# Two plain feed-forward tiles ahead of the Strassen products, sums of token blocks moved behind them

## The chip, the cores and the metric

The kernel runs on one core of a Trainium2 chip. The metric is the device time of one execution in microseconds (us); the median of three runs before the change is 2620.79 us (2618.11 to 2621.23).

## The reference

Two trunk layers of a diffusion backbone, for 128 context tokens and 512 latent tokens (640 columns in all), with a model width of 1024. Each layer is

```
x += 1/2 * gate1 * SwiGLU_1(mod(rmsnorm(x)))
x += gate2 * Mixer(mod(rmsnorm(x)))
x += 1/2 * gate3 * SwiGLU_2(mod(rmsnorm(x)))
```

SwiGLU(h) = (silu(h @ Wg) * (h @ Wu)) @ Wout, with Wg and Wu of 1024 x 2816 and Wout of 2816 x 1024. The mixer of layer 0 is a convolution beside a bidirectional scan (HGRN2), that of layer 1 is windowed attention with grouped keys. The modulation (shift, scale, gate) is a product of a conditioning vector with a 1024 x 9216 matrix for each layer; context tokens have one vector, latent tokens another. All numbers are float32.

## The kernel before

**Layout.** Activations stand transposed: eight tiles of 128 channels by 640 tokens. A float32 product is made of three products of split operands: each operand is a rounded high part (`hi`) and the rest (`lo`), and hi*hi, hi*lo, lo*hi are summed in PSUM. `split_x` (L599) makes the parts: ScalarE casts `hi` (L601), VectorE subtracts for `lo` (L602).

**The feed-forwards.** There are four, called FFN 1 to FFN 4 here (layer 0 first and second, layer 1 first and second), written by `ffn` (L638). The 2816 hidden channels are 22 tiles of 128; each tile is a pair of a gate tile and an up tile. They go in four parts of 6, 6, 6 and 4 pairs, and after each part `project_out` (L762) adds that part's output products to x.

**One pair.** `strassen` (L690) makes a pair by seven products of 12 matmuls (four channel tiles by three split terms), each 320 tokens wide. Its weights are quarters of the pair or sums of quarters (`S`, L704, VectorE), split into `ws`. Its token operands are blocks `B`: 11 and 21 are channel tiles 0 to 3 and 4 to 7 of token half 0 (tokens 320 to 639), 12 and 22 the same of half 1 (tokens 0 to 319), T1 to T4 sums of these. Products 1 and 2 use only blocks 11 and 21 and only gate weights; product 3 uses 22; products 5, 6, 7 and 4 use T1, T2, T3 and T4. Products 1, 6, 7 and 4 add up in a PSUM bank of the ring `b` (three banks), 5 and 3 in ring `c` (two), 2 in ring `a` (one). A plain product of the same pair would be 2 x 2 x 8 x 3 = 96 matmuls against 84.

**Making the blocks.** `norm_chunk` does a token half in two steps: `norm_stats` sums squares on TensorE and spreads the reciprocal root into a PSUM bank `nb` taken from the six `mm` banks; then `norm_pair` (L504), called for q = 0 to 3, makes two channel tiles each of `hf` from x and `nb` (L517 VectorE, L520 ScalarE). For half 0 it splits block 11/21 (`bc`). For half 1 it also makes the sums at once: `t` (L534 VectorE, L535 and L536 GpSimd) and their splits `tc`, `td`, and the split of block 22 (`bd`). Half 0 is made during the last output products of the stage ahead (its last 2 to 7 column tiles are held back for that); half 1 only when they are done.

**The start of a feed-forward.** The first three pairs give products 1 and 2 first, then the others. Weights come by SyncE's queue into four buffers `raw` of 512 KB; a gate load is issued for product 1, the up load for product 5, and a buffer is free when the last sum or split has read it. `load_w` asks for its load 400 instructions ahead of its place. In FFN 1 the first pair's two loads are put ahead of the last two modulation loads (`early`).

**Order.** The scheduler orders each engine's instructions before the run; on the chip each engine takes them in that order.

**Work beside the products.** `plan` and `point` put `mod_step` (load of 512 KB, four VectorE operations) behind pairs and output tiles by shares; `pieces` puts four `mod_piece` (two loads, 16 matmuls in float32, two transposes) behind pairs 0 to 3 of FFN 1, 2 and 3.

**Slots.** Blocks, sums, prefetched weights and the rest lie in 18 single slots and 16 pairs of slots, handed out again when freed. Output products take token chunks by `cut` (L56): 384 and 256 wide when the next norm is a mixer's, 320 and 320 otherwise.

Of the kernel before, what the change touches and what calls it, by code (L numbers as in the profile page):

```python
# [16 lines left out]
P = 128  # L17
# [15 lines left out]
WIDE = T + 45  # L33
# [4 lines left out]
START_PAIRS = 3  # L38
# [42 lines left out]
class Trunk:  # L81
    def __init__(self, ctx, tc, i, o):
        self.tc, self.nc, self.i, self.o = tc, tc.nc, i, o
        pool = lambda name, bufs: ctx.enter_context(tc.tile_pool(name=name, bufs=bufs))
        self.const = pool("const", 1)
        self.xp = pool("xp", 1)
        self.rawp = pool("raw", 4)
        self.wp = pool("w", 6)
        self.stp = pool("st", 6)
        self.slots = pool("slots", 1)  # L90
        self.free_slots, self.free_pairs, self.halves = list(range(N_SLOTS)), list(range(N_PAIRS)), []
        self.freed, self.clock, self.spread_out = collections.defaultdict(int), 0, False
# [9 lines left out]
        self.early = {}  # L102
        self.banks(6, 0, 1)
# [17 lines left out]
    def slot(self, name, dtype=F32, n=T):  # L121
# [3 lines left out]
        if n > T:  # L125
            j = next(j for j in self.free_slots if j < N_WIDE)
            self.free_slots.remove(j)
            self.held[name] = ("slot", j)
            return self.slots.tile([P, WIDE], dtype, tag=f"slot{j}", name=name)[:, :n]
# [11 lines left out]
        if kind == "slot":  # L141
# [3 lines left out]
            return self.slots.tile([P, WIDE if j < N_WIDE else T], dtype, tag=f"slot{j}", name=name)[:, :n]  # L145
# [358 lines left out]
    def norm_pair(self, n, c, pb, q):  # L504
# [9 lines left out]
        for k, col in ((q, (0, 1)[c]), (q + 4, (3, 2)[c])):  # L514
            for s0, sn, g in segments(t0, w):
# [4 lines left out]
                nc.scalar.activation(out=f[:, col, a], in_=f[:, col, a], func=AF.Identity, bias=shift[:, k, g:g + 1])  # L520

        def parts(name, src):
            hi, lo = (self.slot(f"{name}{p}{q}", F32R) for p in ("hi", "lo"))
            view = lambda a: a.rearrange("p (c t) -> p c t", t=HW)
            self.split_x(src, view(hi), view(lo))
            self.operand += [f"{name}hi{q}", f"{name}lo{q}"]
            return [(hi[:, c * HW:(c + 1) * HW], lo[:, c * HW:(c + 1) * HW]) for c in range(2)]

        if c == 0:
            self.B["11", q], self.B["21", q] = parts("bc", f[:, 0:4:3])  # L530
            return
        flat = self.full[q]
        t = self.slot(f"t13_{q}"), self.slot(f"t24_{q}")
# [104 lines left out]
    def ffn(self, l, which, n, last):  # L638
# [12 lines left out]
        def do(j, i):  # L651
            p = pairs.setdefault(j, dict(done=set()))
            for r, nm in enumerate(("gate", "up")):
                if nm not in p and (r == 0 or i not in (1, 2)):
                    p[nm] = self.early.pop((j, nm), None)
                    if p[nm] is None:
                        p[nm] = self.load_w(*self.ffn_first(l, which, j)[r])
            self.strassen(p, j, i, bank, g)

        jobs, ends = [], {}  # L660
        for part, (f0, fn) in enumerate(PARTS):
            js = list(range(f0, f0 + fn))
            if part == 0:
                first = js[:START_PAIRS]
# [4 lines left out]
                nxt = js[START_PAIRS]  # L669
                jobs += [(nxt, 1), (first[-1], 4)] + [(nxt, i) for i in (5, 6, 2, 7, 3, 4)]  # L670
                js = js[START_PAIRS + 1:]
# [19 lines left out]
        if not last:  # L691
            self.norm_chunk(n + 1, 1)

# [68 lines left out]
    def project_out(self, w, xhi, xlo, n, final, last=False):  # L762
# [7 lines left out]
        def tile_chunk(m, c, wt):  # L770
            c0, cw = cut(n + 1)[c]
# [26 lines left out]
        if tail:  # L798
# [4 lines left out]
            for m, wt in zip(ms, wts):  # L803
                yield from tile_chunk(m, 0, wt)
            pb = self.norm_stats(n + 1, 0)
            k = 0
            for j, (m, wt) in enumerate(zip(ms, wts)):
                k1 = (KD * (j + 1)) // tail
                self.norm_part(n + 1, 0, pb, range(k, k1))
                yield from tile_chunk(m, 1, wt)  # L810
# [691 lines left out]
    def run(self):  # L1502
# [8 lines left out]
        for j, q in enumerate((0, 2, 1, 3)):  # L1511
            if j == 3:
                for r, nm in enumerate(("gate", "up")):
                    self.early[0, nm] = self.load_w(*self.ffn_first(0, 0, 0)[r])
            for s in (1, 0):
                self.mod_piece(0, s, q)
            if j % 2:
                for c in range(2):
                    for k in (j - 1, j):
# [86 lines left out]
```

## Time and profile before

| | |
|---|---|
| median of three runs | 2620.79 us |
| profiled execution | 2623.11 us, its span 2621.3 us |
| TensorE (PE) busy | 2466.8 us, 94% |
| VectorE (DVE) busy | 2021.0 us, 77% |
| ScalarE (ACT) busy | 1141.7 us, 44% |
| GpSimd (POOL) busy | 222.7 us, 8% |
| mean granted TensorE clock | 0.966 |
| read from memory | 248.32 MB, 96 GB/s over the span |

Times in rows are us from the start of the span, durations us or ns as marked. "a <- b" behind a wait means that a stood idle until b. PEclk is the granted TensorE clock as a share of 2.4 GHz; there are two levels, 1.00 and 0.50.

### The profile page before, as it was taken

To read this page: it belongs to the slowest core of one execution; us is meant where nothing else is said; L and a number is where in the kernel's file an instruction comes from. 1 tells how busy PE (TensorE), PEld (TensorE's weight loads), DVE (VectorE), ACT (ScalarE), POOL (GpSimd) and SP (SyncE) were. 2 spreads that over 40 slices of the span, in tenths; PEclk is the share of its full clock that TensorE was granted. 3 is DMA by queue.
4 is the path that set the end of the run, shared out by engine and by line. 5 is a ranking of instruction groups with operands and counts; after the bars stand their busy time and mean duration, and the time that the engine had idled before them with its cause. 6 is when DMAs were issued, how large, how long until landed. Compare 5 with 4: busy or idle time off the path is not lost. (4 is left out here: it accounts for less than half of the span.)

```text
span 2621.3 us, 43402 instructions
## 1 busy us (share of the span) xinstructions
PE 2466.8 (94%) x16976; PEld 2368.3 (90%) x16976; DVE 2021.0 (77%) x3816; ACT 1141.7 (44%) x2312; POOL 222.7 (8%) x308
## 2 busy tenths in 40 slices
PE   6899999999989779999996899999999997999999
PEld 4799999998989769999995899999987896999998
DVE  6788888878997668888776788778777768575765
ACT  6425252543234543525255434344555655352533
POOL 1000000104243100000011000000132111000000
PEclk7899999999999889999998899999999998999999
DMA  6453535512111135343441444344310022222222
GB/s 212 137 153 111 151 98 151 150 46 59 53 41 35 45 113 155 105 136 95 139 113 42 146 135 122 114 119 118 112 41 17 22 57 61 85 77 85 80 82 73
DMA packets 378260, 254.52 MB, mean 97 GB/s; under 512 B 9301, under 2 KB 362952, under 8 KB 378056
## 3 DMA queue, kind: packets, MB, share of 16 engines
q1 hardware_dynamic: 373112, 248.35, 32.3%
q10 hardware_dynamic: 4944, 3.41, 0.4%
q8 instruction: 133, 2.18, 0.3%
q14 instruction: 71, 0.58, 0.1%
HBM read 248.32 MB, written 3.41 MB: 96 GB/s over the span
## 5 line engine op out<-in xcount | busy, mean ns | idle before, releaser
L615 PE MATMUL po<-g,whi_o 128*128 128x320 f32 (+2 forms) x2672 | 593.8, 311 | 4.0 <-ACT g L601 2.8
L615 PEld LDWEIGHTS po<-g,whi_o 128*128 128x128 f32 x2672 | 446.6, 188 | 14.4 <-ACT g L601 4.0
L615 PE MATMUL po<-g,wlo_o 128*128 128x320 f32 (+2 forms) x1336 | 412.7, 310 | 0.0
L776 DVE SCALAR_TENSOR_TENSOR x<-po,modG,x 128x128 f32<-128x128 f32 (+3 forms) x480 | 196.7, 435 | 139.9 <-PE po L615 138.4
L601 ACT CAST ws<-S 128x512 fp32r<-128x512 f32 x303 | 188.2, 621 | 253.5 <-DVE S L704 61.9
L349 DVE SCALAR_TENSOR_TENSOR ma<-raw_wm,cond,ma 128x512 f32<-128x512 f32 x357 | 257.9, 750 | 34.1 <-DMA raw_wm<-in_w_mod 33.8
L601 ACT CAST whi_o<-raw_o 128x768 fp32r<-128x768 f32 (+1 forms) x142 | 110.0, 775 | 358.9 <-PE po L615 248.2
L735 PE MATMUL pb<-tdhi,ws 128*128 128x320 f32 x1100 | 247.3, 312 | 9.4 <-DVE st L746 8.3
L602 DVE TENSOR_TENSOR ws<-S,ws 128x512 fp32r<-128x512 f32 x303 | 209.9, 694 | 57.3 <-ACT ws L601 56.9
L615 PEld LDWEIGHTS po<-g,wlo_o 128*128 128x128 f32 x1336 | 251.4, 188 | 0.8 <-issue 0.8
L735 PE MATMUL pa<-bchi,ws 128*128 128x320 f32 x704 | 175.8, 318 | 37.1 <-DVE hf L517 31.4
L735 PEld LDWEIGHTS pb<-tdhi,ws 128*128 128x128 f32 x1100 | 184.8, 190 | 15.9 <-DVE st L746 12.0
L735 PE MATMUL pb<-tdlo,ws 128*128 128x320 f32 x616 | 191.0, 312 | 0.0
L735 PE MATMUL pc<-tchi,ws 128*128 128x320 f32 x616 | 150.0, 324 | 38.3 <-ACT ws L601 33.2
L735 PE MATMUL pb<-bchi,ws 128*128 128x320 f32 x704 | 173.3, 314 | 5.8 <-ACT ws L601 4.8
L735 PE MATMUL pb<-bd,ws 128*128 128x320 f32 x528 | 160.6, 311 | 2.0 <-ACT bd L601 2.0
L405 POOL TENSOR_TENSOR acc<-acc,sq 128x320 f32<-128x320 f32 (+2 forms) x38 | 37.0, 975 | 1463.0 <-ACT sq L404 1462.6
L735 PEld LDWEIGHTS pa<-bchi,ws 128*128 128x128 f32 x704 | 126.2, 195 | 38.8 <-issue 31.9
L735 PEld LDWEIGHTS pc<-tchi,ws 128*128 128x128 f32 x616 | 108.7, 197 | 44.5 <-ACT ws L601 40.4
L602 DVE TENSOR_TENSOR wlo_o<-raw_o,whi_o 128x768 fp32r<-128x768 f32 (+1 forms) x142 | 125.9, 887 | 29.6 <-ACT whi_o L601 19.2
L601 ACT CAST ws<-raw_wg 128x512 fp32r<-128x512 f32 x176 | 108.2, 619 | 82.5 <-PE po L615 56.3
L735 PE MATMUL pc<-bd,ws 128*128 128x320 f32 x792 | 142.5, 311 | 0.0
(472 smaller groups left out, 5841.4 us busy)
## 6 DMA issues: line engine op xcount, KB each, us to landing
raw_wm<-in_w_mod SPq DMA_DIRECT2D x144, 512.0 KB, 3.7
raw_wg<-in_ffn_w_in SPq DMA_DIRECT2D x88, 512.0 KB, 4.1
raw_wu<-in_ffn_w_in SPq DMA_DIRECT2D x88, 512.0 KB, 4.1
raw_o<-in_ffn_w_out SPq DMA_DIRECT2D x96, 384.0 KB, 3.6
raw_o<-in_ffn_w_out SPq DMA_DIRECT2D x32, 256.0 KB, 3.1
raw_z<-in_ev_w_in SPq DMA_DIRECT2D x8, 512.0 KB, 3.8
raw_oq<-in_od_w_in SPq DMA_DIRECT2D x8, 512.0 KB, 4.1
raw_o<-in_od_w_out SPq DMA_DIRECT2D x16, 256.0 KB, 2.9
```

The lines of the kernel that those rows point to most:

```text
L349: nc.vector.scalar_tensor_tensor(out=acc, in0=part, scalar=col, in1=acc, op0=ALU.mult, op1=ALU.add)
L405: nc.gpsimd.tensor_tensor(out=self.acc[:, c0:c0 + n], in0=self.acc[:, c0:c0 + n], in1=sq[:, 0:n], op=ALU.add)
L601: nc.scalar.copy(out=hi, in_=src)
L602: nc.vector.tensor_tensor(out=lo, in0=src, in1=hi.bitcast(F32), op=ALU.subtract)
L615: self.last_mm = nc.tensor.matmul(ps, lhsT=a[k], rhs=b[k][:, c0:c0 + n], start=(k == 0 and j == 0), stop=(k == nk - 1 and j == 2))
L735: nc.tensor.matmul(ps, lhsT=a, rhs=b, start=(i in (1, 5, 2) and k == 0 and t == 0), stop=(k == 3 and t == 2), skip_group_check=True)
L776: nc.vector.scalar_tensor_tensor(out=xs, in0=ps[:, s0 - c0:s0 - c0 + sn], scalar=self.modG[:, n, m, g:g + 1], in1=xs, op0=ALU.mult, op1=AL ...
```

## The change

Every feed-forward makes its first two pairs by plain products: `plain_pair` takes one token half of one pair, 24 matmuls for the gate and 24 for the up tile, each into a bank of the `mm` ring, then silu, multiply and split. In FFN 2 to 4 half 0 of both pairs comes first, then half 1; in FFN 1 pair by pair. `norm_pair` for half 1 now makes `hf` and splits two blocks, 12 and 22; the sums are a new function `norm_sums`, written behind the plain products. Strassen starts with two pairs' products 1 and 2 instead of three, the other 20 pairs as before.

Weights of the first pair are prefetched into slots (`upcoming`, split on arrival) during the held-back output tiles of the stage ahead; in FFN 1 those of both pairs, behind the first two modulation pieces, and the two norm halves go in turn. The second pair's weights are loaded and split whole (128 x 1024). Pieces move two pairs later, and no `mod_step` is put behind pairs 0 to 3.

The six wide slots are 704 instead of 685 columns apart, and a pad of 64 bytes stands ahead of the `st` buffers. Output products of all parts but the held-back tiles, and the whole of the last feed-forward's, are cut 384 and 256.

```diff
-WIDE = T + 45
+WIDE, WIDE_ROOM = T + 45, 704
-START_PAIRS = 3
+PLAIN, EARLY, FIRST_TWO = 2, 2, 2
...
+        self.stp.tile([P, 16], F32, name="pad", bufs=1)
...
         if c == 0:
-            self.B["11", q], self.B["21", q] = parts("bc", f[:, 0:4:3])
+            self.B["11", q], self.B["21", q] = self.parts("bc", q, f[:, 0:4:3])
             return
+        for nm, col in (("12", 1), ("22", 2)):
+            b = self.slot(f"b{nm}_{q}", F32R)
+            self.B[nm, q] = b[:, 0:HW], b[:, HW:]
+            self.split_x(f[:, col], *self.B[nm, q])
+        self.operand.append(f"b22_{q}")
...
+    def norm_sums(self, q):
+
+        nc = self.nc
         flat = self.full[q]
+        f = flat.rearrange("p (c t) -> p c t", t=HW)
         t = self.slot(f"t13_{q}"), self.slot(f"t24_{q}")
         nc.vector.tensor_tensor(out=t[0], in0=flat[:, HW:3 * HW], in1=flat[:, 0:2 * HW], op=ALU.subtract)
         nc.gpsimd.tensor_tensor(out=t[1][:, 0:HW], in0=t[0][:, HW:], in1=f[:, 0], op=ALU.add)
         nc.gpsimd.tensor_tensor(out=t[1][:, HW:], in0=f[:, 3], in1=t[1][:, 0:HW], op=ALU.subtract)
         view = lambda a: a.rearrange("p (c t) -> p c t", t=HW)
-        self.B["T1", q], self.B["T3", q] = parts("tc", view(t[0]))
-        b = self.slot(f"bd{q}", F32R)
-        self.operand.append(f"bd{q}")
-        self.B["22", q] = b[:, 0:HW], b[:, HW:]
-        self.split_x(f[:, 2], *self.B["22", q])
-        self.B["T2", q], self.B["T4", q] = parts("td", view(t[1]))
+        self.B["T1", q], self.B["T3", q] = self.parts("tc", q, view(t[0]))
+        self.B["T2", q], self.B["T4", q] = self.parts("td", q, view(t[1]))
         self.free(f"hf{q}", f"t13_{q}", f"t24_{q}")
...
+        plain = EARLY if n == 0 else PLAIN
+        order = [(j, c) for j in range(plain) for c in range(2)]
+        if n:
+            order.sort(key=lambda x: x[1])
+        weights = {}
+        for j, c in order:
+            if j not in weights:
+                weights[j] = [(self.weights(*x), x[1]) for x in self.ffn_first(l, which, j)]
+            self.plain_pair(j, c, weights[j], g)
+        self.free(*[f"b12_{q}" for q in range(4)])
+        for q in range(4):
+            self.norm_sums(q)
...
             if part == 0:
-                first = js[:START_PAIRS]
+                js = js[plain:]
+                first = js[:FIRST_TWO]
...
+        self.points = self.points[plain:]
...
+    def plain_pair(self, j, c, w, g):
+
+        nc = self.nc
+        banks = []
+        x = [[self.B[b, q][part] for b in (("11", "21"), ("12", "22"))[c] for q in range(4)] for part in range(2)]
+        for (hi, lo), name in w:
+            ps = self.mm("pp")[:, :HW]
+            for i, k in enumerate((0, 1, 4, 5, 2, 3, 6, 7)):
+                for t, (a, b) in enumerate(((hi, x[0]), (hi, x[1]), (lo, x[0]))):
+                    nc.tensor.matmul(ps, lhsT=a[k], rhs=b[k], start=(i == 0 and t == 0), stop=(i == KD - 1 and t == 2))
+            banks.append(ps)
+            if c == 1:
+                self.done(name)
+        s = self.stp.tile([P, HW], F32, tag="st", name="sil")
+        nc.scalar.activation(out=s, in_=banks[0], func=AF.Silu)
+        nc.vector.tensor_tensor(out=s, in0=s, in1=banks[1], op=ALU.mult)
+        self.hidden(g, j, c, s)
...
-                yield from tile_chunk(m, c, wt)
+                yield from tile_chunk(m, c, wt, cut(n + 1) if final and not last else CHUNKS)
...
-            if j == 3:
-                for r, nm in enumerate(("gate", "up")):
-                    self.early[0, nm] = self.load_w(*self.ffn_first(0, 0, 0)[r])
             for s in (1, 0):
                 self.mod_piece(0, s, q)
+            if j == 0:
+                for t in range(EARLY):
+                    self.upcoming += self.ffn_first(0, 0, t)
+                self.prefetch()
...
-        self.pieces = {(*at, j): (*what, j) for at, what in pieces for j in range(4)}
+        self.pieces = {(*at, j + 2): (*what, j) for at, what in pieces for j in range(4)}
...
-                  [IN_SHARE] * fn + [1.0] * (KD if part < len(PARTS) - 1 else KD - TAILS[fn][0])]
+                  [IN_SHARE if f0 + j > 3 else 0.0 for j in range(fn)] + [1.0] * (KD if part < len(PARTS) - 1 else KD - TAILS[fn][0])]
...
+            if (l, which) == (0, 1):
+                self.upcoming = self.ffn_first(1, 0, 0)
...
             if which == 0:
+                self.upcoming = self.ffn_first(l, 1, 0)
                 (self.even_mixer, self.odd_mixer)[l](3 * l + 1)
```

## Rows read from the trace of the kernel before

**Rows 1.** The page, part 1: busy us, share of the span, instructions.

```profile
PE 2466.8 (94%) x16976; PEld 2368.3 (90%) x16976; DVE 2021.0 (77%) x3816; ACT 1141.7 (44%) x2312; POOL 222.7 (8%) x308
```

**Rows 2.** Line 735 alone: stretch, its length, busy us (matmuls), clock, DMA share, GB/s.

```profile
2210.00:2240.00 30.00, 30.00 (x207) 30.00 (x206) 1.00 0.39 114
...
893.00:1013.00 120.00, 81.51 (x485) 76.64 (x486) 0.86 0.31 93
2158.00:2258.00 100.00, 77.32 (x504) 75.64 (x504) 0.90 0.23 66
1383.00:1503.00 120.00, 81.94 (x478) 77.34 (x479) 0.84 0.32 92
38.00:158.00 120.00, 86.36 (x504) 80.47 (x504) 0.87 0.44 131
```

**Rows 3.** Groups of instructions by form: the matmuls of 20 modulation pieces.

```profile
L323 PE MATMUL mps<-raw_wm,cond 128*32 128x256 f32 x320 | 33.2, 468 | 11.0 <-DMA raw_wm<-in_w_mod 8.2 <-DVE modA L379 1.7 <-ACT xsq L279 0.6
```

**Rows 4.** TensorE's waits over the span: us, times, longest.

```profile
PE pc L735 <- ACT ws L601: 33.2, 6, 19.4
PE pa L735 <- DVE hf L517: 31.4, 2, 17.0
```

**Rows 5.** Stretches: length, busy PE, PEld, DVE, ACT, POOL, clock, DMA share, GB/s.

```profile
904.00:930.00 26.00, 8.65 (x37) 7.71 (x37) 19.59 (x39) 17.02 (x37) 9.42 (x8) 0.61 0.00 1
...
2172.00:2197.00 25.00, 5.55 (x25) 5.06 (x24) 18.08 (x29) 13.55 (x29) 8.94 (x8) 0.59 0.03 9
...
970.00:982.00 12.00, 7.02 (x40) 5.08 (x33) 5.44 (x12) 3.38 (x7) 0.00 (x0) 0.72 0.44 131
```

**Rows 6.** Order of time at FFN 2's start: start, us, instruction [idle <- releaser].

```profile
904.64 0.33 PE L459 MATMUL nb<-ident,r_n 128*128 128x64 f32 x2
...
905.01 1.84 DVE L517 SCALAR_TENSOR_TENSOR hf<-x,modA,nb 128x128 f32<-128x128 f32 x6 [0.76 <-PE nb L459]
...
919.66 0.60 PE L735 MATMUL pa<-bchi,ws 128*128 128x320 f32 x1 [14.49 <-DVE hf L517]
```

**Rows 7.** Chain of waits at FFN 4's start: start, us, what.

```profile
2170.58 0.84 DVE t L534
2171.55 0.89 POOL t L535
2172.50 1.33 POOL t L536
...
2175.97 0.84 DVE t L534
...
2192.09 3.76 PE pc L735 x12
```

**Rows 8.** SyncE's queue, waits from 890 to 1000 us; order of time near 975.

```profile
SPq L559 <- DVE S L704: 93.4, 6, 61.4
...
974.76 0.69 DVE L704 TENSOR_TENSOR S<-raw_wu 128x512 f32<-128x512 f32 x1 [2.35 <-DMA raw_wu<-in_ffn_w_in]
```

**Rows 9.** VectorE by form: a whole weight tile's split, a hidden half's.

```profile
L602 DVE TENSOR_TENSOR wlo_z<-raw_z,whi_z 128x1024 fp32r<-128x1024 f32 x8 | 9.8, 1222 | 4.4 <-ACT whi_z L601 4.3
...
L602 DVE TENSOR_TENSOR g<-st,g 128x320 fp32r<-128x320 f32 x176 | 83.3, 488 | 4.4 <-ACT g L601 3.8
```

**Rows 10.** Order of time near 39 us, VectorE and GpSimd.

```profile
39.11 1.35 DVE L602 TENSOR_TENSOR ws<-raw_wg,ws 128x512 fp32r<-128x512 f32 x1
...
42.79 0.68 DVE L602 TENSOR_TENSOR ws<-raw_wg,ws 128x512 fp32r<-128x512 f32 x1
...
39.99 1.19 POOL L536 TENSOR_TENSOR t<-hf,t 128x320 f32<-128x320 f32 x1
```

**Rows 11.** SyncE's queue, waits in the first 60 us.

```profile
SPq L559 <- DVE S L704: 12.2, 1, 12.2
```

**Rows 12.** Line 615 alone: output products 320+320 wide, then 384+256.

```profile
1040.00:1080.00 40.00, 20.39 (x136) 19.64 (x134) 1.00 0.38 109
1525.00:1565.00 40.00, 26.00 (x172) 25.17 (x170) 1.00 0.42 119
```

More of the change, by code (lines that the diff above doesn't have):

```diff
@@ L101, in __init__ @@
         self.full, self.B, self.operand = {}, {}, []
-        self.early = {}
         self.banks(6, 0, 1)
@@ L128, in slot @@
             self.held[name] = ("slot", j)
-            return self.slots.tile([P, WIDE], dtype, tag=f"slot{j}", name=name)[:, :n]
+            return self.slots.tile([P, WIDE_ROOM], dtype, tag=f"slot{j}", name=name)[:, :n]
         never = float("inf")
@@ L144, in slot @@
             self.held[name] = ("slot", j)
-            return self.slots.tile([P, WIDE if j < N_WIDE else T], dtype, tag=f"slot{j}", name=name)[:, :n]
+            return self.slots.tile([P, WIDE_ROOM if j < N_WIDE else T], dtype, tag=f"slot{j}", name=name)[:, :n]
         if kind == "half":
@@ L520, in norm_pair, with parts @@
                 nc.scalar.activation(out=f[:, col, a], in_=f[:, col, a], func=AF.Identity, bias=shift[:, k, g:g + 1])
[L522 to L527, printed above, removed]
         if c == 0:
-            self.B["11", q], self.B["21", q] = parts("bc", f[:, 0:4:3])
+            self.B["11", q], self.B["21", q] = self.parts("bc", q, f[:, 0:4:3])
             return
+        for nm, col in (("12", 1), ("22", 2)):
[3 more added lines that the diff above has]
+        self.operand.append(f"b22_{q}")
+    def parts(self, name, q, src):
+        hi, lo = (self.slot(f"{name}{p}{q}", F32R) for p in ("hi", "lo"))
+        view = lambda a: a.rearrange("p (c t) -> p c t", t=HW)
+        self.split_x(src, view(hi), view(lo))
+        self.operand += [f"{name}hi{q}", f"{name}lo{q}"]
+        return [(hi[:, c * HW:(c + 1) * HW], lo[:, c * HW:(c + 1) * HW]) for c in range(2)]
+    def norm_sums(self, q):
+        nc = self.nc
         flat = self.full[q]
+        f = flat.rearrange("p (c t) -> p c t", t=HW)
         t = self.slot(f"t13_{q}"), self.slot(f"t24_{q}")
@@ L654, in do @@
                 if nm not in p and (r == 0 or i not in (1, 2)):
-                    p[nm] = self.early.pop((j, nm), None)
-                    if p[nm] is None:
-                        p[nm] = self.load_w(*self.ffn_first(l, which, j)[r])
+                    p[nm] = self.load_w(*self.ffn_first(l, which, j)[r])
             self.strassen(p, j, i, bank, g)
+        plain = EARLY if n == 0 else PLAIN
[10 more added lines that the diff above has]
+            self.norm_sums(q)
         jobs, ends = [], {}
@@ L668, in ffn @@
                     jobs += [(nxt, 5), (j, 4), (nxt, 6), (nxt, 3), (nxt, 7)]
-                nxt = js[START_PAIRS]
+                nxt = js[FIRST_TWO]
                 jobs += [(nxt, 1), (first[-1], 4)] + [(nxt, i) for i in (5, 6, 2, 7, 3, 4)]
-                js = js[START_PAIRS + 1:]
+                js = js[FIRST_TWO + 1:]
             jobs += [(j, i) for j in js for i in (1, 5, 6, 2, 7, 3, 4)]
             ends[len(jobs)] = part
+        self.points = self.points[plain:]
         for at, (j, i) in enumerate(jobs):
@@ L768, in weights, with tile_chunk @@
             return (self.split_w_slots if slotted else self.split_w)(raw, f"o{n}_{m}")
-        def tile_chunk(m, c, wt):
-            c0, cw = cut(n + 1)[c]
+        def tile_chunk(m, c, wt, cuts):
+            c0, cw = cuts[c]
             ps = self.mm("po")[:, :cw]
@@ L803, in project_out @@
             for m, wt in zip(ms, wts):
-                yield from tile_chunk(m, 0, wt)
+                yield from tile_chunk(m, 0, wt, cut(n + 1))
             pb = self.norm_stats(n + 1, 0)
@@ L809, in project_out @@
                 self.norm_part(n + 1, 0, pb, range(k, k1))
-                yield from tile_chunk(m, 1, wt)
+                yield from tile_chunk(m, 1, wt, cut(n + 1))
                 if j < slotted:
@@ L1511, in run @@
         for j, q in enumerate((0, 2, 1, 3)):
-            if j == 3:
-                for r, nm in enumerate(("gate", "up")):
-                    self.early[0, nm] = self.load_w(*self.ffn_first(0, 0, 0)[r])
             for s in (1, 0):
                 self.mod_piece(0, s, q)
+            if j == 0:
+                for t in range(EARLY):
+                    self.upcoming += self.ffn_first(0, 0, t)
+                self.prefetch()
             if j % 2:
-                for c in range(2):
-                    for k in (j - 1, j):
+                for k in (j - 1, j):
+                    for c in range(2):
                         self.norm_pair(0, c, pb[c], k)
```

## The prediction

> **What bounds the kernel now.** I read the page's busy table first: TensorE is busy for 94% of the span, VectorE for 77% [rows 1], so TensorE's own work and its standstills are all there is to win. The second view is the busy time of the Strassen products by stretch. In the fourth feed-forward's steady stretch 207 matmuls take 30.00 us, 0.145 us each, at full clock; while the first six pairs are made, the same matmuls are far apart [rows 2]. The stretches hold:
>
> - FFN 2: 485 matmuls, 70.3 us of work, in 120 us. Four modulation pieces of 16 matmuls take 33.2/20 = 1.7 us each [rows 3], 7 us; statistics and transposes I put at 4 us. 120 - 70.3 - 11 = 39 us are lost.
> - FFN 3: 478 matmuls, 69.3 us; 120 - 69.3 - 11 = 40 us lost.
> - FFN 4: 504 matmuls, 73.1 us; no pieces; 100 - 73.1 - 4 = 23 us lost.
> - FFN 1: 504 matmuls, 73.1 us; six pieces, the first output products and the rest, about 15 us; 120 - 73.1 - 15 = 32 us lost, part of it before the operands can be there at all.
>
> The third view, TensorE's waits, names two places: product 2 (`pa`) waiting for VectorE's `hf`, 17.0 us at the longest, and product 5 (`pc`) waiting for ScalarE's `ws`, 19.4 us [rows 4]. The stretches around them show what that costs: PE busy for 8.65 of 26 us in FFN 2 and 5.55 of 25 us in FFN 4, with the granted clock at 0.61 and 0.59, so that after the wait TensorE also runs at its lower level for some microseconds; VectorE is busy for 19.59 and 18.08 us of it [rows 5].
>
> The two waits have different causes. In FFN 2 `pa` has its data and stands from 904.8 to 919.66 for `hf` [rows 6]: the bank of ring `a` is the last of the `mm` ring, which is the bank where `nb` of half 1 lies until VectorE has read it for the last `hf`. FFN 3 repeats it. In FFN 4 the banks are dealt anew, `pa` runs, and the wait is for the sums: the chain goes `t` on VectorE, two adds on GpSimd, split, next `t`, one turn in 5.4 us (2170.58 to 2175.97), four turns for four q, and ends when `pc` starts at 2192.09 [rows 7]. VectorE takes its list in order and the sums `S` of the weights stand behind the last turn.
>
> A third loss follows. The four `raw` buffers stay full of the first pairs' weights until `S` has read them: SyncE's queue waits 93.4 us for that between 890 and 1000, and later an up load lands late [rows 8]; near it PE is busy 7.02 of 12 us at clock 0.72 [rows 5]. There are two such places in FFN 2 and two in FFN 3, between the pieces of the first pairs, about 5 us each: 10 us for each FFN, within the 39 and 40.
>
> **The change part by part.**
>
> *More products.* A plain pair has 96 matmuls against 84: 8 pairs x 12 x 0.145 = +13.9 us, 3.5 us for each feed-forward, all on the path.
>
> *The cover.* At the statistics' end of half 1 in FFN 2 (904.97, the end of `nb` [rows 6]) TensorE had done 36 of the matmuls that need half 0 alone. After the change there are 2 x 96 plain ones and 48 that need no sum (products 1 and 2 of two pairs): 240 - 36 = 204, 29.6 us at full clock, until 934.6. Half of the plain ones (96) need half 1: the first 60 left cover 8.7 us, to 913.7.
>
> *What the cover must hide.* VectorE, from 905.0: `hf`, 16 operations at 1.84/6 [rows 6], 4.9 us; splits of blocks 12 and 22, 8 at 0.488 (the form of a hidden half [rows 9]), 3.9 us; the second pair's weights, 2 at 1.222 [rows 9], 2.4 us: 11.2 us, to 916.2. Blocks 12 and 22 of q = 0 and 1 come in half that time, and the products take them in that order, so half 1's products wait 0 to 3 us; I take 2. Then the sums: four turns of 5.0 us (2170.58 to 2192.09 is 21.5 us with `S` and `ws` behind), and between them the plain pairs' post-work, 4 halves at 2 x 0.488. 916.2 + 20 + 4 is 940; T1, needed first, is there a split earlier, near 938. The cover ends at 934.6 + 2: a stall of 1 to 4 us, and with a clock that has fallen after it, as [rows 5] shows, I take 7 us for both waits of a start. The ends are 0 (turns interleaved with `hf`, as they are now) and the whole of the next part's rival.
>
> *`nb` and the banks.* Eight plain banks are dealt from the `mm` ring; `nb`'s comes sixth, for the up tile of the first pair's half 1, which needs all `hf` anyway. The wait of [rows 6] goes; what is late next is the sums.
>
> *Weights.* The first pair's are split in the tail of the stage ahead, 2 x 1.2 us on VectorE and 1 MB on SyncE's queue ahead of the tail's own tiles. The nearest bound on what that can hold up is that tail's slack: nothing, to 2 x 2.4 us for each of three tails if VectorE sets the pace there; I take 0, since the four `raw` buffers are emptied by a split at once, and keep +7. A plain pair frees its buffers by its split; then two gate and two up loads are all that Strassen's start asks for, four buffers. So the loads no longer queue behind `S`, and with no `mod_step` behind the first pairs I expect half of the 10 us in FFN 2 and 3 to go: -5 each. Pieces and `mod_step` as such are only moved; the longer shares elsewhere lie under steady products, where PE is at 30.00 of 30 us [rows 2].
>
> *FFN 1.* Queue waits of 12.2 us behind `S` [rows 11] fall away, since early weights are split on arrival; 1 MB more is loaded before the last modulation pieces. TensorE gets plain products for the first channel tiles while the rest is loaded. From 32 us lost I take 20, with 3.5 us of added products: net -8. Ends: 0 gained with 3.5 added, +4; and -20.
>
> *Chunks.* 172 output matmuls of 384 and 256 take 26.00 us, 0.151 us; 136 of 320 take 20.39 us, 0.150 [rows 12]. Some 2400 are recut: 0 taken, 0 to +4 us kept, and as much below nothing, since the two rows differ by a count or two at their edges.
>
> *Padding.* It moves addresses; no row sets an operation's time beside its address. The nearest are matmuls of 320 from different slots, 0.145 and 0.150 us [rows 2, 12]: 3%, most of it the edges of the second stretch. Taken as address alone it would be some 50 us over the 10,000 of that width, either way; I take 0, the nearer, and a tenth of it as ends, -5 and +5.
>
> *A rule against the change.* In the first products' time a `ws` split took 1.35 us beside a GpSimd add of 1.19 us, and 0.68 us alone [rows 10]. The Trainium skill (SBUF — State Buffer, the part on ports) says that a VectorE operation with two inputs in SBUF and a GpSimd one that reads SBUF exclude each other; the trace agrees. So the sums, now beside the plain pairs' post-work, slow it: 8 adds x 0.67 us = 5 us of VectorE for each start, which I leave to the rival below.
>
> **Sum.** FFN 2: 39 becomes 3.5 + 7 + 5 = 15.5, -23.5. FFN 3: -24.5. FFN 4: 23 becomes 10.5, -12.5. FFN 1: -8. Together -68 us: the profiled 2623.1 becomes 2555. The median of the runs shown is 2.3 us under the profiled one, so 2553 there.
>
> **The rivals.**
>
> *B, the sums stay behind the plain products.* Their slots may be the ones that the first pair's weights or block 12 leave, or VectorE's list may have the plain post-work first. Then the chain of 21.5 us begins at the plain products' end (904.97 + 156 x 0.145 = 927.6) against 7 us of cover: a gap of 14.5 us and 2 to 3 us of lower clock, 20.5 us with the added products, against some 23 now in a start. For it: the splits of `S` stood so behind the sums [rows 7]. Against: the sums are ready long before. Left are the loads' 10 us, 3 x 2.5 at the starts and nothing in FFN 1: 2605. With the ports' 5 us in FFN 2 to 4 but the sums beside the products, 2570; that lies in the forecast's own range.
>
> *C, slower.* One mechanism: the first `t` is placed behind the post-work of Strassen's first products as well, so that the 21.5 us have no cover. Then each start loses 3.5 + 21.5 + 3 = 28, 5 more than now in FFN 2 to 4, and FFN 1, where the sums now hide under the loads, loses 25 more: less the loads' 10 and FFN 1's queue waits, +20 to +30, 2645. It turns slower when the chain begins later than 2 us after TensorE has run out of other products: 68 us over four starts is 17 us above my 7, 24 in all, and the chain is 21.5. Against it: nothing that waits for a product is needed by `t`.
>
> *D, the change doesn't relieve the loads.* The late loads near the pieces stay: 10 us back and, with 5 us in FFN 1, 2570.
>
> **How the numbers follow.** Forecast with its shades, D among them: 0.77, own range 2530 to 2580. B: 0.12. C: 0.08; something else 0.03. The best case, no stall in a start, no loss at the pieces and FFN 1 at -20, is 68 + 21 + 10 + 12 = 111 less; I count 30 of these 43 us as reachable, which is 2525. To leave 2 in 10 out, the range goes from 2525 to 2605. About 0.2% can be told from no change in this kernel: faster by more than that 0.86 (forecast and most of B), within it 0.05 (the rest of B), slower 0.09.
>
> **What would show it.** Right: no wait of `pa` for `hf`; in each start a single TensorE wait under 8 us, for `ws` or `tc`; `t` of line 534 running while plain products run; the granted clock at 1.00 over most of the starts; SyncE's wait for `S` well under 93 us; 16,976 + 96 matmuls, less or more for the transposes. Wrong: `t` beginning only after the last plain product (B) or after products 1 and 2 (C), VectorE's splits in the tails ahead of FFN 2 to 4 holding up output products, or output products of 384 and 256 that are slower than the row.

## The result and the profile after

The changed kernel takes 2531.73 us (median of 4 runs, 2529.23 to 2533.2) beside 2621.01 us for the kernel before on the same chip: ratio 0.9654, interval 0.9633 to 0.9676. That is 89 us less; forecast were 68. The profiled execution took 2530.51 us, 92.6 less than the one before; its span is 2528.1 us, 93.2 under the one before.

Part 1 of the page after, in the columns of [rows 1]:

```profile
PE 2443.4 (97%) x17072; PEld 2354.8 (93%) x17072; DVE 1985.4 (79%) x3746; ACT 1118.6 (44%) x2274; POOL 224.0 (9%) x308
```

TensorE has the 96 added matmuls and is busy 23 us less: part of what fell away was work at TensorE's lower clock, not only standstill. The trace's clock records have 178 us at that level before and 58 after, without the last microseconds of the span.

TensorE's waits after the change (us in all, times, longest), to be held against [rows 4]:

```profile
PE hgb L457 <- DVE r_hg L437: 10.5, 3, 6.3
PE pa L770 <- DVE st L781: 7.7, 4, 2.2
...
PE pc L770 <- ACT ws L606: 4.2, 3, 1.6
```

`pa` no longer waits for `hf`; `pc`'s longest wait fell from 19.4 to 1.6 us. A wait that the forecast did not name stands now in all four starts: `pa` of the second Strassen pair waits for VectorE to read the one bank of ring `a` (`st`). It isn't new; before the change the view had

```profile
PE pa L735 <- DVE st L746: 5.7, 4, 2.5
```

The order of time in FFN 2 after the change: VectorE's first `t` and `tclo`, its last `t` and the first `S`, then TensorE's two waits (start, us, instruction, idle time before it and releaser):

```profile
900.36 0.82 DVE L543 TENSOR_TENSOR t<-hf 128x640 f32<-128x640 f32 x1 [0.43 <-PE pp L720]
...
902.47 1.50 DVE L607 TENSOR_TENSOR tclo<-t,tchi 128x640 fp32r<-128x640 f32 x1 [0.88 <-ACT tchi L606]
...
916.14 0.82 DVE L543 TENSOR_TENSOR t<-hf 128x640 f32<-128x640 f32 x1
...
918.75 1.19 DVE L739 TENSOR_TENSOR S<-raw_wu 128x512 f32<-128x512 f32 x1
```
```profile
917.41 0.42 PE L770 MATMUL pa<-bchi,ws 128*128 128x320 f32 x1 [1.54 <-DVE st L781]
...
921.05 0.42 PE L770 MATMUL pc<-tchi,ws 128*128 128x320 f32 x1 [1.61 <-ACT ws L606]
```

The last plain products of FFN 2, in the view of tile `pp` (first and last start at its end):

```profile
L720 PE MATMUL pp<-b,wlo_wu x8: 307/308/308, 907.2 to 910.3; 128*128 128x320 f32 x8
```

The sums are made as before, in some 20 us (900.36 to 921.05) and with `S` still behind the last `t`; now TensorE works above them, and the first `t` starts 10 us ahead of the last plain product. The stretches of the four starts, first products to beyond the first output products (length, busy PE, PEld, DVE, ACT, POOL, clock, DMA share, GB/s):

```profile
29.00:149.00 120.00, 113.21 (x808) 100.83 (x801) 92.86 (x184) 56.29 (x119) 9.64 (x8) 0.97 0.52 158
875.00:995.00 120.00, 115.20 (x808) 109.86 (x807) 97.94 (x186) 57.95 (x121) 8.66 (x9) 0.99 0.37 112
1337.00:1457.00 120.00, 113.07 (x797) 108.34 (x796) 94.41 (x182) 56.75 (x118) 8.57 (x8) 0.99 0.37 111
2079.00:2179.00 100.00, 96.80 (x649) 95.60 (x648) 73.64 (x137) 52.90 (x110) 8.57 (x8) 0.97 0.19 54
```

The clock column was 0.87, 0.86, 0.84 and 0.90 before, for line 735's stretches in [rows 2]. SyncE's queue, waits from 870 to 980 us, against [rows 8]:

```profile
SPq L564 <- DVE S L739: 73.0, 4, 62.3
```

It waited 93.4 us before; the longest wait is 62.3 us where it was 61.4. What waited so long was a pair's up load before (the second of the two in the first line) and is a modulation weight now:

```profile
870.04 62.16 SPq L559 DMA_DIRECT2D raw_wu<-in_ffn_w_in  x2
```
```profile
924.88 4.59 SPq L564 DMA_DIRECT2D raw_wm<-in_w_mod  x2
```

To compare kernels I read the times of the matmul records: the length of each start, from a feed-forward's first product to its first output product (FFN 1 from the span's start), in us. "Again" is the changed kernel a second time; the other columns are the experiments below.

```
        before  after  again | bank  sums1  late  share | plain1 plain3 noprefetch third
FFN 1    151.6  131.8  134.5 | 149.9 146.6  139.3 139.6 | 133.0  133.8  129.7      138.8
FFN 2    122.3   95.1   95.4 | 125.5  98.0   95.4 104.3 | 108.0   97.0  106.1       98.4
FFN 3    123.8   94.0   92.6 | 122.0  93.9   93.8  97.2 | 103.8   95.5   99.3       96.5
FFN 4     98.8   86.6   85.6 | 100.6  86.8   86.8  86.5 |  96.2   87.1   92.5       86.0
```

Before to after: -19.8, -27.2, -29.8 and -12.2, together -89.0 of the 93.2 us of span. Of the rest, the mixer ahead of FFN 2 took 366.1 us and not 362.3, that ahead of FFN 4 277.4 and not 282.5; kernels with the same instructions there took 360 to 370 and 276 to 284, so I don't count that to the change. FFN 1's start is 129.7 to 134.5 us long in the five kernels here whose FFN 1 is the same, 132.6 in the mean; the other starts, where the kernels are alike, agree within 1.4, but for FFN 2 in "sums1" (98.0). Each column is one execution; those of "plain1" (2576.17 us) and "third" (2546.86) were the longest of their kernels, 6 and 11 us above the medians.

### The profile page after: what moved, and what is told of

It is laid out like the page before. It is cut to its first block, busy times and chain, and to the rows that moved or that the text cites. A ratio compares the mean times of both kernels' runs of the same rounds, so it can differ in the third digit from the quotient of the medians.

```text
span 2528.1 us, 43467 instructions
## 1 busy us (share of the span) xinstructions
PE 2443.4 (97%) x17072; PEld 2354.8 (93%) x17072; DVE 1985.4 (79%) x3746; ACT 1118.6 (44%) x2274; POOL 224.0 (9%) x308
## 5 line engine op out<-in xcount | busy, mean ns | idle before, releaser
L620 PE MATMUL po<-g,whi_o 128*128 128x256 f32 (+2 forms) x2672 | 585.0, 310 | 2.4 <-DVE st L777 0.9
L620 PEld LDWEIGHTS po<-g,whi_o 128*128 128x128 f32 x2672 | 444.7, 188 | 12.2 <-ACT g L606 2.6
L620 PE MATMUL po<-g,wlo_o 128*128 128x256 f32 (+2 forms) x1336 | 410.5, 308 | 0.4 <-DVE wlo_o L607 0.4
L811 DVE SCALAR_TENSOR_TENSOR x<-po,modG,x 128x256 f32<-128x256 f32 (+3 forms) x480 | 196.4, 434 | 128.5 <-PE po L620 127.0
L770 PE MATMUL pc<-b,ws 128*128 128x320 f32 x1140 | 191.2, 308 | 0.0
L770 PEld LDWEIGHTS pc<-b,ws 128*128 128x128 f32 x1140 | 173.4, 188 | 0.0
L770 PE MATMUL pb<-b,ws 128*128 128x320 f32 x540 | 138.6, 309 | 0.0
L770 PE MATMUL pa<-bchi,ws 128*128 128x320 f32 x560 | 128.3, 310 | 8.1 <-DVE st L781 7.7
L607 DVE TENSOR_TENSOR ws<-raw_wg,ws 128x512 fp32r<-128x512 f32 x160 | 110.2, 691 | 27.0 <-ACT ws L606 26.8
L770 PE MATMUL pb<-bchi,ws 128*128 128x320 f32 x560 | 128.3, 310 | 1.0 <-DVE x L811 1.0
L973 DVE SCALAR_TENSOR_TENSOR cw<-pad,vecs,cw 128x655 f32<-128x655 f32 x120 | 121.4, 1012 | 1.8
```

The lines of the kernel that those rows point to most:

```text
L607: nc.vector.tensor_tensor(out=lo, in0=src, in1=hi.bitcast(F32), op=ALU.subtract)
L620: self.last_mm = nc.tensor.matmul(ps, lhsT=a[k], rhs=b[k][:, c0:c0 + n], start=(k == 0 and j == 0), stop=(k == nk - 1 and j == 2))
L770: nc.tensor.matmul(ps, lhsT=a, rhs=b, start=(i in (1, 5, 2) and k == 0 and t == 0), stop=(k == 3 and t == 2), skip_group_check=True)
L811: nc.vector.scalar_tensor_tensor(out=xs, in0=ps[:, s0 - c0:s0 - c0 + sn], scalar=self.modG[:, n, m, g:g + 1], in1=xs, op0=ALU.mult, op1=AL ...
L973: nc.vector.scalar_tensor_tensor(out=y, in0=x[:, j:j + T + 15], scalar=col(j), in1=y, op0=ALU.mult, op1=ALU.add)
```

## The experiments

Where a difference to the changed kernel is given without a stage, it is that of the ratios to the kernel before (the changed kernel's: 0.9654 in the first comparison, 0.9661 run again; 0.966 is taken) times 2621 us.

**1. The bank alone, in the kernel before.**

```diff
-        ring = {"b": mm[0:3], "c": mm[3:5], "a": mm[5:6]}
+        ring = {"b": mm[0:3], "c": [mm[3], mm[5]], "a": mm[4:5]}
```

> The kernel before with one edit: ring `a` of the Strassen products takes the bank next to last of the `mm` ring, and ring `c` the last, where `nb` of half 1 lies. Theory 1 (the prediction's): the `pa` wait for `hf` in FFN 2 and 3 is this bank, but the sums come next; only the 36 `pa` matmuls of the first three pairs (5.2 us) move into the standstill, and product 5 then waits longer for its sums. The `pa` wait of 17 us goes, FFN 2 and FFN 3 get 3 to 6 us shorter each, FFN 1 and FFN 4 stay: 2609 to 2615 us. Theory 2: the bank is what the start costs, and the sums are ready behind it: 12 to 15 us each, 2591 to 2597 us.

Measured: 2625.68 us beside 2622.93, ratio 1.0011 (0.9996 to 1.0027). TensorE's waits, from the whole span:

```profile
PE pc L735 <- ACT ws L601: 71.0, 6, 20.2
```

The wait for `hf` is gone, and the wait for the sums has become 71.0 us where the two together were 64.6 [rows 4]. Theory 2 falls; of theory 1 the mechanism holds, but not even its 3 to 6 us came. The bank hid the sums' chain and cost nothing beside it that could be told.

**2. FFN 1 with Strassen products from the first pair.**

```diff
-PLAIN, EARLY, FIRST_TWO = 2, 2, 2
+PLAIN, EARLY, FIRST_TWO = 2, 0, 2
...
+            if j == 3:                     # before the last modulation pieces; the first pair takes these
+                for r, nm in enumerate(("gate", "up")):
+                    self.early[0, 0, nm] = self.load_w(*self.ffn_first(0, 0, 0)[r])
...
-                first = js[:FIRST_TWO]
+                two = FIRST_TWO if n else 3
+                first = js[:two]
```

> The changed kernel, but FFN 1 begins with Strassen products from its first pair, three pairs interleaved and the first pair's weights asked for as late as in the kernel before; FFN 2 to 4 as changed. The first six pairs of FFN 1 took 12 us less and its first output products came 21 us earlier than before. Theory 1: the plain products, which need no sums, made all of it: FFN 1 goes back by 18 to 22 us, 2550 to 2554 us. Theory 2: what the change does to the rest of FFN 1 (halves made q by q, no `mod_step` behind the first pairs, wide chunks) made most of it: FFN 1 goes back by 4 to 9 us, 2536 to 2541 us. The prediction had 8 us in all for FFN 1.

Measured: 2543.2 us, ratio 0.9698 (0.9684 to 0.9713), 10 us more. FFN 1's start is 146.6 us long, 14 more than the mean of 132.6. TensorE's waits from 36 to 146 us:

```profile
PE pc L774 <- ACT ws L607: 8.2, 1, 8.2
PE mps L329 <- ACT msb L327: 3.6, 5, 0.9
PE mps L324 <- DMA raw_wm<-in_w_mod: 2.8, 3, 1.4
```

The plain products, with their early request, made at most some 14 of FFN 1's 20 us. The wait of 8.2 us, ahead of the first product 5 at 71.42, is this version's own: the kernel before had that product at 62.05, and its longest wait of `pc` for `ws` in FFN 1 was 2.5 us. Time and stage lie between the two theories.

**3. FFN 1's plain weights asked for later.**

```diff
-            if j == 0:
+            if j == 3:
                 for t in range(EARLY):
                     self.upcoming += self.ffn_first(0, 0, t)
```

> The changed kernel, but the weights of FFN 1's two plain pairs are asked for and split behind the sixth modulation piece and not behind the second (where the kernel before asked for one pair). Theory 1: the early request is half of FFN 1's gain: the first products start 6 to 10 us later, as in the kernel before (38.1 against 29.4 us), and the whole takes 2538 to 2542 us. Theory 2: the queue brings the same bytes in the same time, the modulation weights come earlier instead, and `hf` with them, so that the time stays within 2 us of the changed kernel's 2532.

Measured: 2537.2 us, ratio 0.967 (0.9649 to 0.9691), which overlaps the changed kernel's. The stage tells it better: the first products start at 42.5 us and not at 29.4, the first output products come 7.5 us later, 6.7 later than in the mean of the five. So theory 1, by stage; by the median alone it is not settled.

**4. The planner's shares as before.**

```diff
-                  [IN_SHARE if f0 + j > 3 else 0.0 for j in range(fn)]
+                  [IN_SHARE if f0 + j > 1 else 0.0 for j in range(fn)]
```

> The changed kernel, but the planner gives the third and fourth pair of each part their share of `mod_step` again (0.4, as in the kernel before), and the first two none. FFN 3 gained 31 us where 24.5 were forecast; in FFN 2 and 3 the loads behind the first pairs stood behind the sums `S`. Theory 1: the steps behind those pairs, whose loads and products fall among the modulation pieces, held up the loads: 5 us come back in each of FFN 2 and FFN 3, 2540 to 2544 us, and the TensorE clock falls there again. Theory 2: the plain pairs, which free their load buffers by a split, relieve the loads alone: within 2 us of the changed kernel's 2532.

Measured: 2543.99 us, ratio 0.9705 (0.9689 to 0.9721), 12 us more. By stage, against the first profile of the changed kernel: FFN 1 +7.8, FFN 2 +9.2, FFN 3 +3.2, FFN 4 (which has no steps) -0.1. That is 20 us, but the profiled span is only 9.8 us longer: what lies behind the starts, with fewer steps in it, is shorter, the rest of FFN 1 alone by 4.9. Two stretches of FFN 2, 915 to 935 and 935 to 955, changed kernel and then this one:

```profile
915.00:935.00 20.00, 16.52 (x114) 14.52 (x114) 17.68 (x29) 11.13 (x23) 2.21 (x2) 1.00 0.27 82
935.00:955.00 20.00, 19.43 (x141) 18.40 (x140) 14.13 (x33) 8.92 (x19) 0.00 (x0) 1.00 0.71 208
```
```profile
915.00:935.00 20.00, 16.68 (x100) 15.90 (x99) 17.60 (x28) 10.53 (x21) 4.39 (x4) 0.91 0.16 48
935.00:955.00 20.00, 16.88 (x118) 13.93 (x117) 13.37 (x30) 7.79 (x17) 0.00 (x0) 0.93 0.62 190
```

37 matmuls fewer in 40 us, at a lower clock. SyncE's queue shows part of the reason: the weights of the pairs stand between modulation weights.

```profile
939.24 2.39 SPq L564 DMA_DIRECT2D raw_wm<-in_w_mod  x2
944.91 0.37 SPq L564 DMA_DIRECT2D raw_wu<-in_ffn_w_in  x1
948.05 8.77 SPq L564 DMA_DIRECT2D raw_wm<-in_w_mod  x3
960.30 0.37 SPq L564 DMA_DIRECT2D raw_wg<-in_ffn_w_in  x1
```

In the changed kernel that up load was issued at 937.46 and not at 944.91; here `pc` waits 2.5 us for `ws` at 951.85. Not all of the 9.2 us come from the loads: 1.9 are lost in the first 96 products, ahead of any step, where the lower clock from 887.2 lasts 6.8 and not 3.4 us. Experiment 2, whose FFN 2 has no such steps either, has the same loss there and a start of 98.0, so some 6 us remain for the shares. Theory 1 holds, in FFN 2 with about its 5 us, in FFN 3 with less. FFN 1, of which it said nothing, lost 7.8.

**5 to 8. Padding and wide chunks.** All on one chip: the changed kernel again, without the padding, without the wide chunks, and the kernel before with the padding alone.

```diff
-WIDE, WIDE_ROOM = T + 45, 704
+WIDE, WIDE_ROOM = T + 45, T + 45      # no padding; the "pad" tile left out too
...
-                yield from tile_chunk(m, c, wt, cut(n + 1) if final and not last else CHUNKS)
+                yield from tile_chunk(m, c, wt, cut(n + 1))      # no wide chunks
```

> The changed kernel itself, beside the three kernels on padding and chunks, so that differences of 2 to 10 us between them can be told on one chip. Every theory expects its 2532 us, and start-to-start distances of 146.7 ns for matmuls of 320 columns, 173.5 for 384 and 117.5 for 256.

> The changed kernel without the padding: wide slots of 685 numbers and not 704, no `pad` tile; the instructions are the same. Matmuls of 384 columns follow each other at 173.5 ns in the changed kernel and at 175.7 before, those of 256 at 117.5 and 118.5. Theory 1: the slots' addresses do it: without the padding 2851 x 2.2 + 3656 x 1.0 ns = 9.9 us come back, 2539 to 2542 us, with 175.7 and 118.5 ns. Theory 2: the neighbours of the matmuls do it (more of one width in a row in the wide chunks): 173.5 and 117.5 ns stay, and the time within 2 us of the changed kernel.

> The changed kernel with the output products of the feed-forwards in chunks of 320 and 320 columns again (the padding stays). Theory 1: chunks of 384 and 256 take 173.5 + 117.5 = 291.0 ns a pair of matmuls, two of 320 take 2 x 146.7 = 293.4: over some 1100 pairs the wide ones save 2.6 us, so this takes 2534 to 2535 us. Theory 2 (the prediction's): the two cuts cost the same, within 1 us. Theory 3: wide ones cost more at the chunks' edges, where VectorE takes a longer operation per bank, so this is faster, 2528 to 2531 us.

> The kernel before with the padding alone (wide slots of 704 numbers, the 64-byte `pad` tile); the instructions are the same. Theory 1: addresses set the pace of matmuls of 384 and 256 columns: 1753 x 2.2 + 2568 x 1.0 ns = 6.4 us less at most, 2614 to 2617 us, with 173.5 and 117.5 ns. Theory 2 (the prediction's): nothing, within 2 us of the kernel before, with 175.7 and 118.5 ns.

Ratios to the kernel before on that chip (2623.69 us), and mean start-to-start distances between matmuls of one width, from their records:

```
                  us      ratio (interval)            384      256      320 columns
before          2623.69   1                          175.7 ns 118.5 ns 146.7 ns
before, padded  2617.73   0.9976 (0.9963 to 0.9989)  173.5    117.5    146.7
after again     2533.04   0.9661 (0.9645 to 0.9678)  173.5    117.5    146.7
without padding 2539.10   0.9681 (0.9664 to 0.9699)  176.0    118.5    146.5
320 + 320       2537.83   0.9685 (0.9664 to 0.9705)  173.5    117.5    146.7
```

Line 620 alone (619 without the padding) in FFN 4, 40 us of output products in full flow: the changed kernel, without the padding, and with 320 + 320 (busy PE and matmuls, PEld, clock, DMA share, GB/s):

```profile
2167.00:2207.00 40.00, 40.00 (x276) 39.69 (x275) 1.00 0.26 75
```
```profile
2175.50:2215.50 40.00, 40.00 (x272) 39.70 (x271) 1.00 0.25 73
```
```profile
2185.00:2225.00 40.00, 39.95 (x273) 39.68 (x272) 1.00 0.25 73
```

276 matmuls against 272: the same instructions from other addresses. By the distances a pair of 384 and 256 takes 291.0 ns and not 294.5, 1.2% less, and those of 320 do not gain. Theory 1 on the padding holds as to the distances, in both directions, and a padded kernel before is 6 us faster; which bit of the address does it was not tried. Without the padding the median is 6 us higher, though the intervals overlap; the +0.5 us in each of the first three of FFN 4's output parts, and +0.3 in the fourth, agree with it. The wide chunks are a gain only with the padding: 173.5 + 117.5 = 291.0 ns against 293.4 for two of 320, and 294.5 without it. Their 4.8 us in the median are not settled, for the same reason; the distances and the counts 276 against 273 speak for theory 1.

**9 and 10. One plain pair, and three, in FFN 2 to 4.**

```diff
-PLAIN, EARLY, FIRST_TWO = 2, 2, 2
+PLAIN, EARLY, FIRST_TWO = 1, 2, 2      # the other run: 3, 2, 2
```

> The changed kernel with one plain pair at the start of FFN 2, 3 and 4 in place of two (FFN 1 keeps two). In the changed kernel's FFN 2 the first product that needs a sum starts at 921.05 us, after waits of 1.5 and 1.6 us; what it needs last is done at about 921. Theory 1: the cover decides. TensorE has 96 matmuls, 14 us, less ahead of the sums, the chain ends 3 us sooner for two halves less of post-work: a wait of about 13 us in each of the three starts, 9 to 10 more than now, and some 3 us of lower clock, less 1.7 us for 12 matmuls: +10 each, 2558 to 2566 us, with a `pc` wait of 10 us or more. Theory 2: what helped is the order of the sums and the relieved loads, and one pair covers enough: -2 each, 2524 to 2530 us.

> The changed kernel with three plain pairs at the start of FFN 2, 3 and 4 (FFN 1 keeps two; the first modulation piece follows the plain pairs). Theory 1: two pairs cover all but the last 2 us; a third takes 12 matmuls more, 1.7 us, and removes at most the 1.6 us wait for `ws`: within 3 us of the changed kernel's 2532. Theory 2: the waits of 1.5 and 1.6 us and the low clock behind them go, 4 us in each start for 1.7: 2523 to 2527 us. Theory 3: operands stay longer in their slots and the third pair's weights come through two more splits by VectorE beside the sums: 2537 us or more.

Measured with one: 2570.27 us, ratio 0.9801 (0.9784 to 0.9818). FFN 2, 3 and 4 are 12.6, 11.2 and 10.6 us longer than in the changed kernel run again. TensorE's waits, and FFN 2's in the order of time with VectorE's last `t` and first `S`:

```profile
PE pc L770 <- ACT ws L606: 40.9, 3, 14.9
```
```profile
922.73 0.63 PE L770 MATMUL pc<-tchi,ws 128*128 128x320 f32 x1 [12.97 <-ACT ws L606]
```
```profile
916.59 0.82 DVE L543 TENSOR_TENSOR t<-hf 128x640 f32<-128x640 f32 x1
921.34 0.68 DVE L739 TENSOR_TENSOR S<-raw_wu 128x512 f32<-128x512 f32 x1
```

Theory 1 holds: 13 us of wait for 14 us of cover taken away. Counted from FFN 2's first product (875.69 us with two pairs, 880.18 with one), the first product with a sum starts after 45.4 and after 42.6 us: the chain ended 2.8 us sooner, near the 3 that theory 1 had.

With three (the first modulation piece now stands behind the plain products): 2539.07 us, ratio 0.9683 (0.9669 to 0.9696), 6 us more, with intervals that overlap. The three starts hold 1.6 + 2.9 + 1.5 of it by stage. TensorE's waits in FFN 2, 870 to 975 us:

```profile
PE pc L773 <- ACT ws L606: 1.4, 1, 1.4
PE mps L328 <- ACT msb L326: 1.2, 1, 1.2
PE pp L723 <- ACT whi_wu L606: 1.1, 1, 1.1
PE pc L773 <- DVE ws L607: 0.4, 1, 0.4
```

The waits of `pa` and `pc` ahead of the sums are gone, but others stand in their place: `pp` for the split of the third pair's weights (1.1 us in each of the three starts) and `pc` later on, at 960.34. The waits of FFN 2's start are 4.1 us in all with two pairs and with three. So theory 2 falls, although its waits went. What is added is theory 1's, the matmuls, 3 x 1.76 = 5.3 us; what keeps the waits from growing shorter is in part theory 3's, the third pair's splits; and the time is theory 3's. Two pairs have the lowest median of the three numbers tried; between two and three the time does not decide.

**11. No early request for the first pair's weights in FFN 2 to 4.**

```diff
-            if (l, which) == (0, 1):
-                self.upcoming = self.ffn_first(1, 0, 0)
...
-                self.upcoming = self.ffn_first(l, 1, 0)
```

> The changed kernel, but the first pair's weights of FFN 2, 3 and 4 are asked for at the start of the feed-forward and not in the tail of the stage ahead. The prediction had 0 to +7 us as the price of the early request and nothing as its worth. Theory 1: without it the two splits, 2 x 1.2 us, stand behind `hf` on VectorE and the load behind the tail's: each start loses 3 to 8 us, 2541 to 2556 us. Theory 2: the queue runs ahead anyhow and the splits fit in: within 3 us of 2532. Theory 3: the tails were held up by it: 2525 to 2528 us.

Measured: 2552.57 us, ratio 0.9732 (0.9719 to 0.9746), 19 us more; the starts of FFN 2, 3 and 4 are 10.7, 6.7 and 6.9 us longer than in the changed kernel run again. The waits:

```profile
PE pc L770 <- ACT ws L606: 22.4, 3, 11.0
```

and VectorE in FFN 2, the split that moved into the start, the first `t` and the first `S`:

```profile
898.73 1.22 DVE L607 TENSOR_TENSOR wlo_wu<-raw_wu,whi_wu 128x1024 fp32r<-128x1024 f32 x1 [1.72 <-ACT whi_wu L606]
...
906.25 0.82 DVE L543 TENSOR_TENSOR t<-hf 128x640 f32<-128x640 f32 x1 [1.14 <-PE pp L720]
...
926.40 0.68 DVE L739 TENSOR_TENSOR S<-raw_wu 128x512 f32<-128x512 f32 x1
```

Counted from FFN 2's first product (873.62 us here, 875.69 in the changed kernel), the first `t` starts 8.0 us later and the first `S` 9.7, although the cover is whole. Theory 1 holds, in FFN 2 with more than its 8 us.

**12. A third pair's product 1 in the gap of `pa`.**

```diff
-                jobs += [(j, i) for j in first for i in (1, 2)]
+                nxt = js[FIRST_TWO]
+                jobs += [(first[0], 1), (first[0], 2), (first[1], 1), (nxt, 1), (first[1], 2)]
...
-                jobs += [(nxt, 1), (first[-1], 4)] + [(nxt, i) for i in (5, 6, 2, 7, 3, 4)]
+                jobs += [(first[-1], 4)] + [(nxt, i) for i in (5, 6, 2, 7, 3, 4)]
```

> The changed kernel, but product 1 of the third Strassen pair (12 matmuls that need no sum) stands between products 1 and 2 of the second, where `pa` now waits 1.5 to 2.5 us for its one bank to be read. Theory 1: those 1.7 us fill that wait and move the first product with a sum back by as much, so that both waits of a start go: -2 to -4 us in each of four starts, 2518 to 2526 us. Theory 2: a third gate tile fills the fourth `raw` buffer, the second pair's up tile is asked for later, and what is won in the start is lost behind it, as it was in the kernel before: 2530 to 2540 us.

Measured: 2535.78 us, ratio 0.9666 (0.9652 to 0.9679): no gain that can be told. TensorE's waits in FFN 2, 885 to 985 us, against the longest three after (880 to 975):

```profile
PE pc L770 <- ACT ws L606: 2.5, 3, 1.6
PE mps L323 <- DMA raw_wm<-in_w_mod: 0.5, 1, 0.5
PE pc L770 <- DVE ws L607: 0.2, 1, 0.2
```
```profile
PE pc L770 <- ACT ws L606: 1.6, 1, 1.6
PE pa L770 <- DVE st L781: 1.5, 1, 1.5
PE mps L328 <- ACT msb L326: 1.3, 2, 0.7
```

`pa`'s wait is gone, the waits for `ws` have grown, and all waits of the view together are 3.2 us against 4.8; still the starts of FFN 2 and 3 are 3 to 4 us longer than in the changed kernel run again (and FFN 1's 6 us longer than the mean), in an execution 11 us above the median. What makes them longer these waits don't show. Theory 1 falls. SyncE's wait for `S` there is 76.3 us and not 73.0, which fits theory 2 but doesn't show it. No version tried beats the changed kernel.

## Why the prediction came out as it did

The time fell into the range, 21 us under the forecast: 12 of these in FFN 1, 4 in FFN 2 and 5 in FFN 3. Step by step:

- **The cover and the chain: right.** `t` runs beside plain products, the `pa` wait for `hf` is gone, and what is late next is the sums, as the forecast said; experiments 1 and 9 show both sides (the bank alone gives nothing, 14 us less of cover bring 13 us of wait). B and C fall with the first `t` at 900.36, ahead of the last plain product at 910.3. What the forecast took for the waits of a start, 7 us, was too much: 1.5 + 1.6 in FFN 2. The clock is 0.97 to 0.99 over the starts, not quite the 1.00, and the matmuls are 96 more, as said.
- **FFN 2: -23.5 forecast, -27.2 measured. FFN 3: -24.5 forecast, -29.8 measured.** Worked out as in the forecast but over the start itself, with the matmuls at 0.1467 us, 7 us for pieces and 4 for the rest: before, 122.3 - 504 x 0.1467 - 11 = 37.4 were lost in FFN 2 and 38.9 in FFN 3 (forecast 39 and 40). After, 95.1 - 528 x 0.1467 - 11 = 6.6 and 5.5 are lost, where the forecast left 12. The term that was mis-sized is what stays: 7 us of waits and 5 of late loads. Experiment 4 shows what emptied the second: no `mod_step` behind the first pairs, worth some 6 us in FFN 2 and 3 in FFN 3 (forecast 5 each). D falls. That the pieces stand two pairs later, and that Strassen starts with two pairs and not three, no run took apart.
- **SyncE's wait for `S` "well under 93 us": wrong.** 73.0. The Strassen pairs still fill four buffers until `S` reads them. The load that waits longest behind them is now one for a modulation piece and no longer a pair's.
- **FFN 4: -12.5 forecast, -12.2 measured.** The only start with neither pieces nor steps, and the cleanest test of cover against chain. That the figures meet so closely is luck: 98.8 - 73.9 - 4 = 20.9 us were lost before (forecast 23) and 86.6 - 77.5 - 4 = 5.1 are lost after (forecast 7), two errors of 2 us that cancel.
- **FFN 1: -8 forecast, -19.8 measured (-17 to -22 in the kernels with the same FFN 1).** The step that failed is "from 32 us lost I take 20", which took the loads for a floor. Its end of -20 was the truth. Experiment 2 gives at most 14 us to the plain products (some 7 of it, experiment 3, to their early request: TensorE starts at 29.4 and not at 38.1 us), and experiment 4 gives 7 to the shares, of which the rest of FFN 1 pays 4.9 back. The clock belongs to it: from 18.4 to 55.9 us it was at the lower level for all but 3.4 us before, and after only from 20.2 to 30.5 and from 37.3 to 44.1.
- **Early requests in the tails: costed at 0 with +7 as the end, no worth named.** Their price was indeed not seen, but they carry 7 to 11 us of each start in FFN 2 to 4 (experiment 11): without them the cover is whole and the chain starts later. The forecast relied on this and should have priced it.
- **Padding: 0 taken, -5 to +5 kept.** About -6 in the kernel before, by the padding alone, just beyond the end. **Chunks: 0 taken.** By distances some 2 to 3 us saved, and only with the padding. They lie outside the starts, where the net is 93.2 - 89.0 = 4.2 us. There the products of the second part of FFN 2 and 3, where moved steps now lie, take 76.4 and 78.0 us and not 74.7 and 76.2; with the shares as before (experiment 4) they take 75.3 and 75.8.
- **The ports: seen, and hidden for the most part.** In the start of FFN 2 `S` at 918.75 took 1.19 us beside GpSimd's add (918.05, 1.34 us), and the next ones 0.68 to 0.69 alone. The Trainium skill (SBUF — State Buffer, Who interferes with whom) says that a VectorE operation with two inputs in SBUF and a GpSimd one that reads SBUF exclude each other, and the trace agrees. VectorE's operations beside the four turns' adds took 3.4 us more there than the same forms alone (the forecast put 5 to the rival); no run took the adds away, but all that `pc` still waits is 1.6 us.

## What to carry over

When an engine waits for a chain on two others, don't ask what it waits for but how much work it has that needs none of the chain: take the chain's length from the trace, count the cover in instructions, and add cover until it just reaches the chain's end (here two pairs: one less cost 37 us; one more gained nothing, its median is 6 us higher). A freed wait shows its worth only where nothing equally late stands behind it, as with the bank. And count a start's losses between two events of the work, with all the matmuls between them: over round stretches the forecast's losses were 1 to 2 us too high.

## Unexpected in the hardware

Matmuls of 384 and 256 columns follow each other at 175.7 and 118.5 ns, or at 173.5 and 117.5 ns when their operands' slots lie elsewhere, moved by the 64-byte `pad` tile and the wider slots (704 numbers in place of 685); those of 320 keep 146.5 to 146.7 ns either way. Which of the two matters, and which operand's address it is, no run here told apart.
